# Starting the recurrent heads inside the second half's projections, one step per half tile, matmuls kept in program order

## The chip, the cores and the metric

The kernel runs on one core of one Trainium2 chip. The metric is device time in microseconds (us) of one execution; lower is better. Before the change three runs took 2574.16, 2576.18 and 2580.22 us, median 2576.18.

## The reference, cut to what matters

One inference step of a two-layer hybrid decoder, model width 1024, for 512 prompt rows and 8 sample rows (520 columns in the kernel). A layer is a half-step SwiGLU FFN, a token mixer and another half-step FFN, each followed by a residual layer norm. The mixer projects its input with one wide matrix and splits the columns among sliding-window attention, a Mamba-2 branch and HGRN2, a gated linear recurrence; each branch is projected, gated, summed, and projected once more.

The change is about HGRN2, which has 4 heads of width 128:

```
qh = silu(q);  f = lb + (1 - lb) * sigmoid(f_logit);  kh = (1 - lb) * sigmoid(-f_logit)
o_t = q_t . S_t        with  S_t = diag(f_t) S_(t-1) + k_t i_t^T      (per head, 512 steps)
y = rmsnorm(o) * silu(g)
```

The 512 steps are worked out in blocks instead of one by one: products of f inside blocks of 8, then pair products q k^T in five levels of block sizes 8, 8, 16, 32 and 64 with q and k rescaled between levels, then a state for each 128 steps. The 8 sample rows take one step each from a stored state.

## The kernel before, in words

Activations lie transposed: 8 tiles of 128 features by 520 columns, in two halves of 260 columns. Every large product is done in three matmuls on a high and a low part (`gemm`, L177 to L179), 8 tiles deep, so one unit of output (128 columns of the weight) for one half is 24 matmuls: a "half tile". A weight tile is 512 KB; it is loaded by a DMA on SP's queue (L87), and split into high part by ScalarE (L90) and low part by VectorE (L91).

An instruction's place in its engine's queue is settled at compile time by a scheduler that follows dependencies and priorities; `early(k)` raises the priority of what is traced inside it as if it had been traced some thousand instructions sooner (`EARLY`). At run time each engine works through its queue in order, and an instruction waits on semaphores for its inputs. `keep_in_program_order` adds an order, without a semaphore, between an instruction and the one traced before it on its engine.

In `mixer` (L557) the work around the change is:

- `hgrn_lin` (L601) projects 16 units: 0 to 3 are the four f_logit tiles T (identity evacuation, L517), then for each head q (SiLU, L526 to L528), i (identity) and g (SiLU). The ten units of `MIX_HEAD` (L501) are done for the first half of the columns, and then all ten for the second half, with their weight tiles loaded again; `ln_rest` puts the second half of the layer norm behind the third unit. The other six units, and then six units of `attention_lin` (L1083), have both halves in one go.
- `weave` (L585) takes one full unit of projections per round, and behind it, under `early(3)`, `pace` steps of every live head. A head is a generator (`hgrn_head`, L633), and a step is what lies between two `yield`s. `HG_ROUNDS` and `HG_SAMPLES` say in which round a head, or a sample head (`hgrn_sample`, L760), begins. Before, the rounds begin behind both halves of `MIX_HEAD`: 12 rounds of two steps each.
- A head's steps: **setup** (two sigmoids on ScalarE, L639 and L640, scalings on VectorE, a chain of 6 and one of 5 products on POOL, L652 and L655, and a reciprocal, L653); **scaling** of q and k (L660, L661) into `hep` and `hk`; **levels**, each 8 matmul instructions into a bank of tag "s" (L678), a masked copy (L693, L688 or L683), and a rescaling of both operands for the next level (L697 and L698 behind level 0, L705 and L706 behind the others); **transposes** of i and k (L717, L718); the **state** (L724, L725, L728); the **output** (L735, L738), its norm (L743 to L746); its **transpose** (L754), gating (L756) and split.
- A sample head copies its columns (L765), transposes them (L769), stores them to DRAM (L773, r8d), reads them back spread over the partitions (L779), and updates the state on POOL and VectorE (L780 to L789).
- `merge` (L1273) for branch 0 comes next; its second product needs the split outputs of all four heads.

Tag "s" has 3 PSUM banks, tag "g" of the projections 4, and a head's wide tiles come from 8 slots (`sum_slot`).

Of the kernel before, what the change touches and what calls it, by code (L numbers as in the profile page):

```python
# [15 lines left out]
AF = mybir.ActivationFunctionType  # L16
# [3 lines left out]
P = 128  # L20
# [23 lines left out]
HK = DT // 2  # L44
HG_ROUNDS = (0, 2, 4, 5)
AT_ROUNDS = (0, 0, 3, 3)
HG_SAMPLES = (5, 6, 8, 10)

# [77 lines left out]
class Kernel:  # L126
# [373 lines left out]

    MIX_HEAD = (0, 1, 2, 3, 4, 5, 6, 7, 8, 9)  # L501

# [3 lines left out]

    def lin(self, evac, m=P, halves=(0, 1)):
        wt = self.w.get()
        for half in halves:
            c0, c1 = HALVES[half]  # L510
            p = self.bank()
            self.gemm(p, wt, self.xs, half, m=m)
            with self.early(1):
                evac(p[:m, : c1 - c0], c0, c1)

    def lin_bias(self, out, bias, scale=1.0, halves=(0, 1)):
        self.lin(lambda p, c0, c1: self.nc.scalar.activation(out[:, c0:c1], p, AF.Identity, bias=bias, scale=scale), halves=halves)  # L517

    def lin_silu(self, out, hbias, halves=(0, 1)):

        nc = self.nc

        def evac(p, c0, c1):
            u = self.half_tile()[:, : c1 - c0]
            t = self.half_tile()[:, : c1 - c0]
            nc.scalar.activation(u, p, AF.Identity, bias=hbias, scale=0.5)  # L526
            nc.scalar.activation(t, p, AF.Tanh, bias=hbias, scale=0.5)
            nc.vector.scalar_tensor_tensor(out[:, c0:c1], t, 1.0, u, op0=ALU.add, op1=ALU.mult)  # L528

        self.lin(evac, halves=halves)  # L530

# [25 lines left out]
    def mixer(self, l):  # L557
# [5 lines left out]
        lins = self.hgrn_lin(l)  # L563
# [5 lines left out]
        pair = lambda i: self.attention_pair(l, i, aq)  # L569

        starts = [(r, head(h)) for h, r in enumerate(HG_ROUNDS)] + [(r, smp(h)) for h, r in enumerate(HG_SAMPLES)]
        self.weave(lins, starts, 22 - len(self.MIX_HEAD), 2)
        with self.early(3):
# [25 lines left out]


    def hgrn_lin(self, l):  # L601
        nc = self.nc
        pr, dp, sp = self.par[l], self.dp[l], self.sp
        T = [self.slot(name="hT") for _ in range(HGH)]
        q, it, sg = {}, {}, {}

        def unit(u, halves=(0, 1)):
            hb = dp[:, u : u + 1]
            if u < 4:
                self.lin_bias(T[u], pr[:, 48 + u : 49 + u], halves=halves)  # L610
                return
            h, kind = (u - 4) // 3, (u - 4) % 3
            d, n = ((q, "hq"), (it, "hi"), (sg, "hsg"))[kind]
            if h not in d:
                d[h] = self.slot(name=n)
            if kind == 1:
                self.lin_bias(d[h], pr[:, 48 + u : 49 + u], halves=halves)
            else:
                self.lin_silu(d[h], hb, halves)

        for half in (0, 1):
            for u in self.MIX_HEAD:
                unit(u, (half,))
                if half == 0 and u == 2:
                    self.ln_rest()
        yield T, q, it, sg
        for u in range(16):
            if u in self.MIX_HEAD:
                continue
            unit(u)  # L630
            yield

    def hgrn_head(self, l, h, st):  # L633
# [36 lines left out]
        def level(i):  # L670
# [42 lines left out]
        for src, dst in ((it[h], itok), (ks, ktok)):  # L713
            p = self.bank("s")
            for c in range(4):
                cs = slice(c * P, (c + 1) * P)
                nc.tensor.transpose(p[:, cs], src[:, cs], self.ident)  # L717
            nc.scalar.copy(dst[:, :TP], p)  # L718
# [3 lines left out]
        for c in range(4):  # L722
            cs = slice(c * P, (c + 1) * P)
            nc.tensor.matmul(pst[:, cs], lhsT=ktok[:, cs], rhs=itok[:, cs], start=True, stop=True)  # L724
        nc.vector.tensor_copy(st[:, :P], pst[:, :P])  # L725
# [7 lines left out]
        for c in range(4):  # L733
            cs = slice(c * P, (c + 1) * P)
            nc.tensor.matmul(po[:, cs], lhsT=att[:, c, :], rhs=itok[:, cs], start=c == 0, stop=False)  # L735
        for c in range(1, 4):
            cs, ps = slice(c * P, (c + 1) * P), slice((c - 1) * P, c * P)
            nc.tensor.matmul(po[:, cs], lhsT=qp[:, cs], rhs=st[:, ps], start=False, stop=c == 3)  # L738
        o = self.sum_slot("ho")[:, :TP]
# [9 lines left out]
        )  # L749
        yield  # L750
        pt = self.bank("s")
        for c in range(4):
            cs = slice(c * P, (c + 1) * P)
            nc.tensor.transpose(pt[:, cs], o[:, cs], self.ident)  # L754
        yv = self.sum_slot("hy")[:, :TP]
# [4 lines left out]
    def hgrn_sample(self, l, h, st):  # L760
# [3 lines left out]
        for n, t in zip(("q", "i", "sg"), st[1:]):  # L764
            nc.vector.tensor_copy(sp[n][:, sl], t[h][:, TP:])  # L765

        p = self.bank("x")
        for k, n in enumerate(("f", "k", "q")):
            nc.tensor.transpose(p[:8, k * P : (k + 1) * P], sp[n][:, sl], self.ident)  # L769
        r8 = self.sm(3 * P, "r8", rows=8)  # L770
# [111 lines left out]
    def mamba(self, l):  # L882
# [16 lines left out]
        for j in range(4):  # L899
            self.lin_silu(z[j], dp[:, 28 + j : 29 + j])  # L900
            nc.vector.tensor_copy(self.sp["z"][:, 8 * j : 8 * j + 8], z[j][:, TP:])
# [181 lines left out]
    def attention_lin(self, l, aq):  # L1083
        nc = self.nc
        pr = self.par[l]
        k = self.slot(name="ak")
        self.lin_bias(k, pr[:, 48 + 16 : 48 + 17])
        nc.vector.tensor_copy(self.sp["ak"][:, :8], k[:, TP:])
        nc.sync.dma_start(self.ap["o_pk"][l], k[:, TP - P : TP])
        yield  # L1090
        v = self.slot(name="av")
        self.lin_bias(v, pr[:, 48 + 17 : 48 + 18])
# [3 lines left out]
        yield  # L1096
        for i in range(4):
            q = self.slot(name="aq")
            self.lin_bias(q, self.qb[l][:, i : i + 1], scale=0.125)
            nc.vector.tensor_copy(self.sp["aq"][:, 8 * i : 8 * i + 8], q[:, TP:])  # L1100
            aq[i] = q
            yield

# [456 lines left out]
```

## Time and profile before

| | |
|---|---|
| three runs, median | 2576.18 us (2574.16 to 2580.22) |
| profiled execution | 2577.91 us, of which 2576.1 us are the span from first to last instruction |
| mean granted TensorE clock | 0.993 |
| TensorE matmul, weight load | 98%, 96% of the span |
| VectorE, ScalarE, POOL | 76%, 49%, 27% |
| DMA | 318 MB, mean 124 GB/s |

The two layers run one after the other. In layer 0 the mixer's projections begin near 369 us, their second half near 399, and the first merge near 540; in layer 1 the same work comes 1278 us later. In the profile's names, `g` and `s` are PSUM banks by tag, `hk` a head's scaled key, `hep` its scaled query, `hst` its state, `smp` and `s_q` to `s_sg` tiles of the samples, `wh` and `wl` the weight parts. A wait row says which engine and line waited, on which engine's tile and line, for how long in total, how often, and the longest.

### The profile page before, as it was taken

What the parts mean: (1) busy time and instruction counts of PE and PEld (TensorE: products, weight loads), DVE (VectorE), ACT (ScalarE), POOL (GpSimd) and SP (SyncE); (2) the same over time, 40 slices, a digit from 0 to 9 for tenths busy, and PEclk for the clock granted to TensorE, in tenths of its full rate; (3) what the DMA queues carried; (4) which work ended last, traced back from release to release, by engine and by line L of the source; (5) the groups of instructions that cost most, each with busy time, mean ns of one, the idle gap of its engine ahead of it and who ended that gap; (6) DMA issues with size and microseconds to landing.
All of it is one profiled execution on the core that took longest, in us unless ns stands there. A gap on an engine that the chain in (4) does not pass through costs nothing.

```text
span 2576.1 us, 51903 instructions
## 1 busy us (share of the span) xinstructions
PE 2513.6 (98%) x20784; PEld 2471.3 (96%) x20784; DVE 1948.8 (76%) x3690; ACT 1255.2 (49%) x2366; POOL 694.1 (27%) x645
## 2 busy tenths in 40 slices
PE   8999999999999999999999999999999999999997
PEld 8999999899989999999989999998999899899997
DVE  8795988865594598858897858988646846979596
ACT  6352566444534463435563434764445345635255
POOL 2121243400143432312331212433001434412124
PEclk9999999999999999999999999999999999999999
DMA  6332356522342433232542414564233433433233
GB/s 210 106 127 76 130 180 217 153 67 89 114 133 85 138 129 110 83 115 90 194 126 85 146 57 145 172 222 140 70 104 99 129 99 128 132 101 119 79 120 119
DMA packets 134066, 318.17 MB, mean 124 GB/s; under 512 B 20452, under 2 KB 56516, under 8 KB 133824
## 3 DMA queue, kind: packets, MB, share of 16 engines
q1 hardware_dynamic: 133824, 314.86, 37.6%
q8 instruction: 163, 2.67, 0.4%
q14 instruction: 79, 0.65, 0.1%
HBM read 302.93 MB, written 11.88 MB: 122 GB/s over the span
## 4 chain that ended last, share of the span: by engine, by line
PE 73%; DVE 15%; DMA 4%; issue 3%; POOL 3%; ACT 2%; SPq 0%; POOLq 0%; ACTq 0%; DVEq 0%
PE g L178 15%; PE g L177 15%; PE g L179 15%; PE g L409 6%; PE g L411 5%; PE g L410 5%; DVE wl L91 3%; PE s L409 2%; PE s L411 2%; PE s L410 2%; DMA ws<-in_w_gu 1%; DVE y L249 1%; DMA smp<-r8d 1%; DVE xl L253 1%; DVE wl L74 1%
## 5 line engine op out<-in xcount | busy, mean ns | idle before, releaser
L177 PE MATMUL g<-xh,wh 128*128 128x260 f32 (+1 forms) x2336 | 668.4, 287 | 6.7 <-ACT xh L1423 5.7
L178 PE MATMUL g<-xl,wh 128*128 128x260 f32 (+1 forms) x2336 | 668.3, 286 | 3.6 <-DVE xl L253 2.7
L179 PE MATMUL g<-xh,wl 128*128 128x260 f32 (+1 forms) x2336 | 667.6, 286 | 1.9 <-DVE wl L91 1.9
L90 ACT CAST wh<-ws 128x1024 fp32r<-128x1024 f32 (+1 forms) x382 | 390.0, 1025 | 348.7 <-PE g L178 228.8
L91 DVE TENSOR_TENSOR wl<-ws,wh 128x1024 fp32r<-128x1024 f32 (+1 forms) x382 | 466.2, 1223 | 109.2 <-ACT wh L90 108.2
L177 PEld LDWEIGHTS g<-xh,wh 128*128 128x128 f32 (+1 forms) x2336 | 438.5, 188 | 10.2 <-ACT xh L1423 5.7
L178 PEld LDWEIGHTS g<-xl,wh 128*128 128x128 f32 (+1 forms) x2336 | 438.4, 188 | 9.3 <-DVE xl L253 4.2
L179 PEld LDWEIGHTS g<-xh,wl 128*128 128x128 f32 (+1 forms) x2336 | 438.7, 188 | 6.5 <-DVE wl L91 3.4
L73 ACT CAST wh<-ws 128x1024 fp32r<-128x1024 f32 (+1 forms) x288 | 265.4, 942 | 300.4 <-PE g L178 161.8
L179 PE MATMUL g<-hh,wl 128*128 128x260 f32 x1408 | 395.9, 283 | 0.0
L178 PE MATMUL g<-hl,wh 128*128 128x260 f32 x1408 | 395.7, 283 | 0.0
L177 PE MATMUL g<-hh,wh 128*128 128x260 f32 x1408 | 392.6, 283 | 1.9 <-DVE y L275 1.9
L74 DVE TENSOR_TENSOR wl<-ws,wh 128x1024 fp32r<-128x1024 f32 (+1 forms) x288 | 321.1, 1121 | 86.9 <-ACT wh L73 85.6
L105 POOL TENSOR_TENSOR ws<-ws 128x512 f32<-128x512 f32 x72 | 132.3, 1837 | 635.1 <-DMA ws<-in_w_gu 281.8
L179 PEld LDWEIGHTS g<-hh,wl 128*128 128x128 f32 x1408 | 264.8, 188 | 0.2
L177 PEld LDWEIGHTS g<-hh,wh 128*128 128x128 f32 x1408 | 262.7, 188 | 2.4 <-DVE y L275 2.3
L178 PEld LDWEIGHTS g<-hl,wh 128*128 128x128 f32 x1408 | 264.7, 188 | 0.1
L409 PE MATMUL g<-xh,wh 128*128 128x260 f32 x864 | 245.8, 285 | 2.9 <-ACT wh L73 2.5
L410 PE MATMUL g<-xl,wh 128*128 128x260 f32 x864 | 243.8, 283 | 0.0
L411 PE MATMUL g<-xh,wl 128*128 128x260 f32 x864 | 241.5, 282 | 1.9 <-DVE wl L74 1.9
L409 PEld LDWEIGHTS g<-xh,wh 128*128 128x128 f32 x864 | 163.3, 189 | 5.8 <-ACT wh L73 4.4
L409 PE MATMUL g<-sx,wh 128*128 128x260 f32 x576 | 164.2, 285 | 4.3 <-ACT wh L73 4.3
(411 smaller groups left out, 5727.5 us busy)
## 6 DMA issues: line engine op xcount, KB each, us to landing
ws<-in_w_gu SPq DMA_DIRECT2D x208, 512.0 KB
ws<-in_w_in SPq DMA_DIRECT2D x132, 512.0 KB
ws<-in_w_dn SPq DMA_DIRECT2D x96, 512.0 KB
ws<-in_w_out SPq DMA_DIRECT2D x32, 512.0 KB
ws<-in_w_dn SPq DMA_DIRECT2D x32, 384.0 KB
smp<-r8d SPq DMA_DIRECT2D x48, 256.0 KB
ws<-in_w_br SPq DMA_DIRECT2D x24, 512.0 KB
smp<-in_hgr SPq DMA_DIRECT2D x16, 256.0 KB
```

Source lines behind the costliest of these rows:

```text
L73: nc.scalar.copy(h[:, :n], s[:, :n])
L74: nc.vector.tensor_tensor(lo[:, :n], s[:, :n], h[:, :n].bitcast(F32), op=ALU.subtract)
L90: nc.scalar.copy(h[:, :n], s[:, :n])
L91: nc.vector.tensor_tensor(lo[:, :n], s[:, :n], h[:, :n].bitcast(F32), op=ALU.subtract)
L105: nc.gpsimd.tensor_tensor(pa[:, b], u[:, a], u[:, b], op=ALU.add)
L177: nc.tensor.matmul(out, lhsT=h[:, wc], rhs=xh[:, c0:c1], start=st, stop=False)
L178: nc.tensor.matmul(out, lhsT=h[:, wc], rhs=xl[:, c0:c1], start=False, stop=False)
L179: nc.tensor.matmul(out, lhsT=lo[:, wc], rhs=xh[:, c0:c1], start=False, stop=en)
L249: nc.vector.scalar_tensor_tensor(y, y, gn, rb, op0=ALU.mult, op1=ALU.mult)
L409: nc.tensor.matmul(out, lhsT=h[:, wc], rhs=xh, start=first and k == 0, stop=False, **go)
L410: nc.tensor.matmul(out, lhsT=h[:, wc], rhs=xl, start=False, stop=False, **go)
L411: nc.tensor.matmul(out, lhsT=lo[:, wc], rhs=xh, start=False, stop=k == HK - 1, **go)
```

## The change

The heads and samples are woven in from the second half of `MIX_HEAD` on. A round is now a half tile and takes one step of each live head: 10 + 24 = 34 rounds. The `lin` helpers become generators that yield behind every half tile. Heads begin in rounds 2, 6, 10 and 15, samples in 14, 18, 22 and 27. `MIX_HEAD` is reordered so that head 0's q, i and g come right behind its T, and head 1's behind these. A head has two empty steps between setup and scaling, a new step border between level 0 with its rescaling and level 1, and two empty steps ahead of the last transpose; a sample has a new border between copies and transposes. All matmuls and transposes of heads and samples go through `keep_in_program_order`. No instruction is added or removed.

```diff
-HG_ROUNDS = (0, 2, 4, 5)
+HG_ROUNDS = (2, 6, 10, 15)
-HG_SAMPLES = (5, 6, 8, 10)
+HG_SAMPLES = (14, 18, 22, 27)
...
-    MIX_HEAD = (0, 1, 2, 3, 4, 5, 6, 7, 8, 9)
+    MIX_HEAD = (0, 4, 5, 6, 1, 7, 8, 9, 2, 3)
...
-    def lin(self, evac, m=P, halves=(0, 1)):
+    def lin(self, *args, **kw):
+        for _ in self.lin_steps(*args, **kw):
+            pass
+
+    def lin_steps(self, evac, m=P, halves=(0, 1)):
...
                 evac(p[:m, : c1 - c0], c0, c1)
+            yield
...
-        self.weave(lins, starts, 22 - len(self.MIX_HEAD), 2)
+        self.weave(lins, starts, len(self.MIX_HEAD) + 2 * (22 - len(self.MIX_HEAD)), 1)
+        for _ in lins:
+            pass
...
+    def mm(self, *args, **kw):
+        self.tc.keep_in_program_order(self.nc.tensor.matmul(*args, **kw))
+
+    def tr(self, *args):
+        self.tc.keep_in_program_order(self.nc.tensor.transpose(*args))
...
-        for half in (0, 1):
-            for u in self.MIX_HEAD:
-                unit(u, (half,))
-                if half == 0 and u == 2:
-                    self.ln_rest()
+        for u in self.MIX_HEAD:
+            for _ in unit(u, (0,)):
+                pass
+            if u == self.MIX_HEAD[2]:
+                self.ln_rest()
         yield T, q, it, sg
+        for u in self.MIX_HEAD:
+            yield from unit(u, (1,))
         for u in range(16):
-            if u in self.MIX_HEAD:
-                continue
-            unit(u)
-            yield
+            if u not in self.MIX_HEAD:
+                yield from unit(u)
...
             nc.gpsimd.tensor_tensor(rv[:, :, a], f[:, :, b], rv[:, :, b], op=ALU.mult)
+
+        yield
+        yield
         yield
         qp, ks = self.sum_slot("hep")[:, :TP], ks[:, :TP]
...
-                nc.tensor.matmul(
+                self.mm(
                     out.rearrange("p (b w) -> p b w", w=w) if i else out,
...
         nc.vector.tensor_tensor(em3, em3, ts.unsqueeze(2).to_broadcast([P, 64, 8]), op=ALU.mult)
         w = 8
+        yield
         for i in range(1, 5):
...
             op=ALU.mult,
         )
         yield
+        yield
+        yield
         pt = self.bank("s")
...
             nc.vector.tensor_copy(sp[n][:, sl], t[h][:, TP:])
+        yield
 
         p = self.bank("x")
```

The other matmuls and transposes of `hgrn_head` and `hgrn_sample` change to `self.mm` and `self.tr` in the same way, and `attention_lin` and the z projections of `mamba` call the generators.

## Rows read from the trace of the kernel before

**Rows 1.** The page, part 1: busy time, share of the span and instructions of each engine.
```profile
PE 2513.6 (98%) x20784; PEld 2471.3 (96%) x20784; DVE 1948.8 (76%) x3690; ACT 1255.2 (49%) x2366; POOL 694.1 (27%) x645
```

**Rows 2.** TensorE's waits, whole kernel: us in total, times, longest us.
```profile
PE s L678 <- DVE hk L698: 7.2, 5, 2.5
...
PE s L678 <- DVE hk L706: 4.0, 6, 1.2
...
PE x L769 <- DVE s_q L765: 2.3, 2, 1.2
...
PE s L738 <- DVE hst L725: 1.5, 2, 1.0
...
PE s L678 <- DVE s_sg L765: 0.8, 1, 0.8
...
PE s L724 <- ACT hkt L718: 0.5, 1, 0.5
PE s L754 <- DVE ho L746: 0.4, 1, 0.4
```

**Rows 3.** Stretches of both layers: us, busy us (instructions) by engine, granted clock, DMA share, GB/s.
```profile
400.00:560.00 160.00, 152.12 (x1262) 148.64 (x1262) 124.20 (x315) 81.71 (x225) 49.92 (x62) 0.99 0.51 157
500.00:530.00 30.00, 27.54 (x224) 26.55 (x223) 26.13 (x78) 12.18 (x42) 5.77 (x5) 0.94 0.44 135
530.00:560.00 30.00, 30.00 (x254) 29.92 (x253) 15.45 (x54) 13.39 (x35) 1.04 (x2) 1.00 0.23 73
514.00:517.40 3.40, 3.40 (x20) 2.82 (x19) 3.32 (x10) 1.48 (x10) 0.00 (x0) 0.51 0.15 30
...
1678.00:1838.00 160.00, 151.20 (x1268) 148.01 (x1268) 124.92 (x315) 82.69 (x226) 50.00 (x62) 1.00 0.50 158
```

**Rows 4.** TensorE's timeline, 511 to 515.5: start, us, line, tiles, count [idle before <- releaser].
```profile
512.38 1.08 PE L678 MATMUL s<-hep,hk 128*128 128x64 f32 x8 [2.46 <-DVE hk L698]
...
513.47 0.28 PE L177 MATMUL g<-xh,wh 128*128 128x260 f32 x1
513.59 0.28 PE L178 MATMUL g<-xl,wh 128*128 128x260 f32 x1
...
514.49 0.42 PE L178 MATMUL g<-xl,wh 128*128 128x260 f32 x1
514.70 0.42 PE L179 MATMUL g<-xh,wl 128*128 128x260 f32 x1
```

**Rows 5.** The same table for instructions of L177 alone (8 in each half tile).
```profile
398.60:450.80 52.20, 34.01 (x120) 22.40 (x119) 1.00 0.74 235
...
398.60:553.90 155.30, 87.33 (x306) 57.74 (x305) 0.99 0.52 161
```

**Rows 6.** VectorE's timeline, 393 to 397: end of the layer norm.
```profile
395.08 0.88 DVE L253 SCALAR_TENSOR_TENSOR xl<-y,par,xh 128x260 fp32r<-128x260 f32 x2
```

**Rows 7.** Timelines of ACT and VectorE, 402 to 416: head 0's setup.
```profile
402.65 0.47 ACT L517 ACTIVATE hT<-g,par 128x260 f32<-128x260 f32 x1
...
415.45 0.43 DVE L661 TENSOR_TENSOR hk<-hk,hrv 128x256 f32<-128x256 f32 x1 [0.52 <-POOL hrv L655]
```

**Rows 8.** VectorE's and POOL's timelines, 428 to 431, and L705's instructions of the whole kernel.
```profile
428.70 1.20 DVE L705 TENSOR_TENSOR hep<-hep,tw 128x256 f32<-128x256 f32 x1
...
428.32 1.30 POOL L780 TENSOR_TENSOR smp<-smp 128x512 f32<-128x512 f32 x1
...
L705 DVE TENSOR_TENSOR hep<-hep,tw x32: 410/418/1495, 428.7 to 1807.4; 128x256 f32<-128x256 f32 x32
```

**Rows 9.** VectorE's groups, 400 to 560: line, tiles, count, busy us, mean ns, idle before.
```profile
L91 DVE TENSOR_TENSOR wl<-ws,wh 128x1024 fp32r<-128x1024 f32 x25 | 31.0, 1244 | 4.2 <-ACT wh L90 4.2
L783 DVE SCALAR_TENSOR_TENSOR smp<-smp,s_i 128x128 f32<-128x128 f32 x32 | 9.5, 352 | 5.5 <-POOL smp L780 2.9 <-DMA smp<-r8d 2.6
...
L528 DVE SCALAR_TENSOR_TENSOR hsg<-ht 128x260 f32<-128x260 f32 x7 | 3.2, 457 | 3.7 <-ACT ht L527 3.7
```

**Rows 10.** SP's timeline, 421 to 422: DMA issues.
```profile
421.34 0.35 SPq L773 DMA_DIRECT2D r8d<-r  x1
```

More of the change, by code (lines that the diff above doesn't have):

```diff
@@ L514, in lin @@
                 evac(p[:m, : c1 - c0], c0, c1)
+            yield
     def lin_bias(self, out, bias, scale=1.0, halves=(0, 1)):
-        self.lin(lambda p, c0, c1: self.nc.scalar.activation(out[:, c0:c1], p, AF.Identity, bias=bias, scale=scale), halves=halves)
+        return self.lin_steps(
+            lambda p, c0, c1: self.nc.scalar.activation(out[:, c0:c1], p, AF.Identity, bias=bias, scale=scale), halves=halves
+        )
     def lin_silu(self, out, hbias, halves=(0, 1)):
@@ L528, in evac @@
             nc.vector.scalar_tensor_tensor(out[:, c0:c1], t, 1.0, u, op0=ALU.add, op1=ALU.mult)
-        self.lin(evac, halves=halves)
+        return self.lin_steps(evac, halves=halves)
     def split(self, y, name, slot=None):
@@ L609, in unit @@
             if u < 4:
-                self.lin_bias(T[u], pr[:, 48 + u : 49 + u], halves=halves)
-                return
+                return self.lin_bias(T[u], pr[:, 48 + u : 49 + u], halves=halves)
             h, kind = (u - 4) // 3, (u - 4) % 3
@@ L616, in unit @@
             if kind == 1:
-                self.lin_bias(d[h], pr[:, 48 + u : 49 + u], halves=halves)
-            else:
-                self.lin_silu(d[h], hb, halves)
-        for half in (0, 1):
-            for u in self.MIX_HEAD:
-                unit(u, (half,))
-                if half == 0 and u == 2:
-                    self.ln_rest()
+                return self.lin_bias(d[h], pr[:, 48 + u : 49 + u], halves=halves)
+            return self.lin_silu(d[h], hb, halves)
+        for u in self.MIX_HEAD:
[3 more added lines that the diff above has]
+                self.ln_rest()
         yield T, q, it, sg
+        for u in self.MIX_HEAD:
+            yield from unit(u, (1,))
         for u in range(16):
-            if u in self.MIX_HEAD:
-                continue
-            unit(u)
-            yield
+            if u not in self.MIX_HEAD:
+                yield from unit(u)
     def hgrn_head(self, l, h, st):
@@ L716, in hgrn_head @@
                 cs = slice(c * P, (c + 1) * P)
-                nc.tensor.transpose(p[:, cs], src[:, cs], self.ident)
+                self.tr(p[:, cs], src[:, cs], self.ident)
             nc.scalar.copy(dst[:, :TP], p)
@@ L723, in hgrn_head @@
             cs = slice(c * P, (c + 1) * P)
-            nc.tensor.matmul(pst[:, cs], lhsT=ktok[:, cs], rhs=itok[:, cs], start=True, stop=True)
+            self.mm(pst[:, cs], lhsT=ktok[:, cs], rhs=itok[:, cs], start=True, stop=True)
         nc.vector.tensor_copy(st[:, :P], pst[:, :P])
@@ L734, in hgrn_head @@
             cs = slice(c * P, (c + 1) * P)
-            nc.tensor.matmul(po[:, cs], lhsT=att[:, c, :], rhs=itok[:, cs], start=c == 0, stop=False)
+            self.mm(po[:, cs], lhsT=att[:, c, :], rhs=itok[:, cs], start=c == 0, stop=False)
         for c in range(1, 4):
             cs, ps = slice(c * P, (c + 1) * P), slice((c - 1) * P, c * P)
-            nc.tensor.matmul(po[:, cs], lhsT=qp[:, cs], rhs=st[:, ps], start=False, stop=c == 3)
+            self.mm(po[:, cs], lhsT=qp[:, cs], rhs=st[:, ps], start=False, stop=c == 3)
         o = self.sum_slot("ho")[:, :TP]
@@ L753, in hgrn_head @@
             cs = slice(c * P, (c + 1) * P)
-            nc.tensor.transpose(pt[:, cs], o[:, cs], self.ident)
+            self.tr(pt[:, cs], o[:, cs], self.ident)
         yv = self.sum_slot("hy")[:, :TP]
@@ L765, in hgrn_sample @@
             nc.vector.tensor_copy(sp[n][:, sl], t[h][:, TP:])
+        yield
         p = self.bank("x")
         for k, n in enumerate(("f", "k", "q")):
-            nc.tensor.transpose(p[:8, k * P : (k + 1) * P], sp[n][:, sl], self.ident)
+            self.tr(p[:8, k * P : (k + 1) * P], sp[n][:, sl], self.ident)
         r8 = self.sm(3 * P, "r8", rows=8)
@@ L899, in mamba @@
         for j in range(4):
-            self.lin_silu(z[j], dp[:, 28 + j : 29 + j])
+            for _ in self.lin_silu(z[j], dp[:, 28 + j : 29 + j]):
+                pass
             nc.vector.tensor_copy(self.sp["z"][:, 8 * j : 8 * j + 8], z[j][:, TP:])
@@ L1086, in attention_lin @@
         k = self.slot(name="ak")
-        self.lin_bias(k, pr[:, 48 + 16 : 48 + 17])
+        yield from self.lin_bias(k, pr[:, 48 + 16 : 48 + 17])
         nc.vector.tensor_copy(self.sp["ak"][:, :8], k[:, TP:])
         nc.sync.dma_start(self.ap["o_pk"][l], k[:, TP - P : TP])
-        yield
         v = self.slot(name="av")
-        self.lin_bias(v, pr[:, 48 + 17 : 48 + 18])
+        yield from self.lin_bias(v, pr[:, 48 + 17 : 48 + 18])
         nc.vector.tensor_copy(self.sp["av"][:, :8], v[:, TP:])
@@ L1095, in attention_lin @@
         aq["k"], aq["v"] = k, v
-        yield
         for i in range(4):
             q = self.slot(name="aq")
-            self.lin_bias(q, self.qb[l][:, i : i + 1], scale=0.125)
+            yield from self.lin_bias(q, self.qb[l][:, i : i + 1], scale=0.125)
             nc.vector.tensor_copy(self.sp["aq"][:, 8 * i : 8 * i + 8], q[:, TP:])
             aq[i] = q
-            yield
     def by_group(self, t):
```

## The prediction

> **What bounds the kernel now.** The page's engine line comes first [rows 1]: TensorE is busy 2513.6 of 2576.1 us, so only its idle time, some 62 us, and any time at a low clock can be won; the change removes no matmul. The waits of TensorE over the whole kernel come next [rows 2]. Seven of the entries belong to the recurrent heads (L678, L724, L738, L754) and their samples (L769): 7.2 + 4.0 + 2.3 + 1.5 + 0.8 + 0.5 + 0.4 = 16.7 us. The table of stretches puts them [rows 3]: between the mixer's second-half projections and the first merge TensorE is busy 152.12 of 160 us in layer 0 and 151.20 of 160 in layer 1, so 7.88 + 8.80 = 16.7 us are idle there, the same sum. VectorE is busy 124.20 of 160 in that stretch, but 26.13 of 30 where the heads are densest and 15.45 of 30 behind that. So the stage is TensorE's, held up in places where a head's matmul stands in its queue before VectorE has finished the input.
>
> TensorE's timeline shows such a place [rows 4]: the second level of a head waits 2.46 us for L698, and behind it the spacing of the projections' matmuls goes from 0.12 to 0.21-0.22 us. The stretch from 514.0 to 517.4 has a granted clock of 0.51, the 1.2 GHz level [rows 3]: at half speed its 3.4 us held 1.7 us of work, so 1.7 us were lost.
>
> **The change, part by part.** A half tile is 24 matmuls at 0.12 us [rows 4], 2.9 us. The projections' second half begins near 398.7 us, and L177 (8 in a half tile) counts the half tiles since then [rows 5]: head 1's first level stands at 120 / 8 = 15, head 3's last transpose (553.9) at 306 / 8 = 38. The stretch of 155 us holds 918 of these matmuls and about 36 of the merge, 114 us; less 7.9 us idle and 1.7 us of low clock, the heads' own matmuls take some 31 us, 7.8 a head. The change keeps them all; only their places and the waits in front of them count.
>
> *Order of the projections.* Units 4, 5, 6 now follow unit 0. In the first half this brings one or two SiLU evacuations (two ACTIVATE of 0.47 us, one VectorE operation of 0.42) ahead of the rest of LN's second half. The last xl of LN ends at 395.96 [rows 6], 2.7 us before TensorE needs the second half. I cost it at nothing; if that margin is gone, at most 1.4 us a layer. The weights are listed in the same order, with the same number of loads.
>
> *Heads' setup.* Head 0's chain from its T (evacuated at 402.65) through ACT's table load, the six and five POOL products, to its scaled key ends at 415.88 [rows 7], 17.2 us after the second half begins. Under the new plan level 0 of head 0 comes behind seven half tiles, 20.2 us. The two empty steps cover it, at cost 0; without them level 0 would stand behind five half tiles, 14.4 us, and wait some 3 us.
>
> *The levels.* Every head now has a half tile between level 0 with its two scalings (L697, L698) and level 1. The five waits for L698 make 7.2 us and the longest is 2.5 [rows 2], shorter than a half tile: I take all 7.2 off. Between later levels VectorE has a masked copy, L705 and L706, three operations like L705's median of 0.42 us [rows 8], 1.3 us together, and often a weight split of 1.24 [rows 9]; 2.5 us just fit into 2.9. Of the 4.0 us for L706 I take half off, 2.0. The waits for hst, hkt and ho (1.5 + 0.5 + 0.4) lie behind longer chains; half off, 1.2.
>
> *Samples.* The new step between their copies and their transposes takes off the two waits for s_q, 2.3, and the one for s_sg, 0.8. Their DMAs move past weight loads on SP's in-order queue: layer 0's first r8d store was issued at 421.34 [rows 10] and can now come only behind half tile 16, some 453 us. That is eleven DMAs a head, moved out of the part in which each half tile loads its own weight tile. The seven entries already make the stage's whole idle time [rows 2, 3], so none of it is a wait for weights and the loads have slack; cost 0. Were that cover gone, a weight load held behind a sample's read would cost a few us once a layer. POOL's two products per half sample (one took 1.3 us [rows 8]) move likewise; only the sample waits for them.
>
> *Pins.* They are an order and no semaphore: a head's matmul may not stand ahead of the projections traced before it, but may stand behind later ones. Each adds nothing of its own. What stands behind a late one is the whole of TensorE's queue, as before.
>
> *Low clock.* It followed the 2.46 us wait; with that gone, 1.7 us come back.
>
> *What is late next.* The plan wants the heads earlier: head 1's level 0 behind 11 half tiles instead of 15, head 3's end behind 30 instead of 38. VectorE's load per head is at most (124.2 - 31.0 - 9.5 - 5.9) / 4 = 19.5 us, the stage less weight splits, sample products and 13 SiLU operations at 0.457 us, 7 of which the row shows [rows 3, 9], or 1.3 us for each of 15 rounds. In rounds 15 to 20 three heads are live: 3.9 us, half a split (0.6), SiLU and samples (0.5), 5.0 us of VectorE against 2.9 + 3 x 7.8 / 15 = 4.4 us of TensorE. That is 0.6 us short in each of six rounds, 3.6 us a layer if nothing slips and 0 if the plan's matmuls slip behind later projections; I take 3 a layer, nearer the first because the matmuls already stood ahead of their inputs before. Sum: -7.2 - 2.0 - 1.2 - 2.3 - 0.8 - 1.7 + 6 = **-9.2 us**. Bounds of the whole: all waits and the low clock gone, -18.4; from above, the second rival.
>
> The profiled execution took 2577.9 us, 1.8 beyond its span and 1.7 above the median of 2576.2. I set the difference against the median: 2567.
>
> **The rivals.** *No binding pin, no change.* All bounds but head 0's first lie earlier than where the matmuls stood, so a pin that only forbids moving ahead may bind nothing: the queue's order is again what the scheduler thinks ready, and VectorE is again late by the same 5%. For it: head 1's level 0 stood four half tiles behind its new bound without any pin [rows 5]. Against: the steps that waited longest get a half tile each. The samples' 3.1 us go, new waits give about as much back: 2574 to 2578, near 2576.
>
> *VectorE takes over (slower).* The place is rounds 15 to 20, where the heads' scalings, the weight splits and POOL's products of the next head meet. For it: VectorE was busy 87% in the densest stretch [rows 3], and L705 took 1.20 us at 428.70, while POOL worked from 428.32 on, instead of its usual 0.42 [rows 8]. If the named waits only change their names, the 16.7 us stay and 3.6 us a layer are added: 2576 + 7 = 2583, and up to 3 us more if each layer gets a low-clock stretch of its own. It decides once VectorE is busy over some 97% of those six rounds. Against: a third of VectorE's time was free in the 30 us behind the dense part.
> The Trainium skill, page "SBUF — State Buffer", section "Who interferes with whom", says that a VectorE instruction with two SBUF inputs contends with a GpSimd instruction that reads SBUF, and its section "SBUF: two separate sides" calls the shared port pair a lock held for the whole instruction. L705 has two such inputs, and its 1.20 us beside POOL's product agree; by that rule alone, packing one head's POOL setup beside two others' levels speaks against the change, towards this rival's time.
>
> **How the numbers follow.** Two runs of this kernel can be told apart at about 0.2%, 5.2 us. The forecast, 2559 to 2571, gets 0.53; no change 0.25; VectorE's rival 0.22. The forecast lies on the side of faster; a weak form of the second and third falls within 0.2%. So faster 0.53, same 0.26, slower 0.21. The range takes the forecast's best side to 2559 and goes up into the third case, to 2584, leaving some 2 in 10 out.
>
> **What would show it.** Right: no wait of L678 for L698 left above 0.5 us, none of L769 for s_q; TensorE idle in the two stages 8 us or less instead of 16.7; no low clock there; the last head transpose near half tile 30 to 34. Wrong: waits of L678 for L706 or L697 of several us between half tiles 15 and 25 with VectorE at 97% or more (the third case), or the levels at the same half tiles as before with the same waits (the second). A new wait of a projection on xl at the start of the second half would show the cost of the new unit order; one on wl, a weight load held on SP's queue.

## The result and the profile after

The kernel after took 2599.72 us (2595.84 to 2604.40, four runs) and the kernel before 2577.73 on the same chip: a ratio of 1.0081, 95% interval 1.0067 to 1.0095. It is slower by some 21 us, above the range and on the other side of the forecast. The profiled execution took 2596.74 us, with a span of 2595.0 against 2576.1, 18.9 us more.

First the table of stretches in layer 0 (us, busy us and instructions of PE, PEld, DVE, ACT, POOL, then granted clock, DMA share, GB/s), of the kernel before and then of the one after:
```profile
400.00:520.00 120.00, 112.12 (x923) 108.94 (x923) 100.92 (x233) 64.59 (x181) 48.89 (x60) 0.99 0.60 185
520.00:580.00 60.00, 60.00 (x493) 59.13 (x492) 37.50 (x132) 27.29 (x75) 1.04 (x2) 1.00 0.20 65
```
```profile
400.00:520.00 120.00, 118.24 (x1007) 116.56 (x1006) 97.94 (x242) 65.00 (x162) 35.30 (x53) 1.00 0.45 146
520.00:580.00 60.00, 49.94 (x363) 45.28 (x363) 36.16 (x131) 27.68 (x102) 12.79 (x9) 0.86 0.44 136
...
532.40:535.80 3.40, 3.40 (x18) 3.40 (x17) 2.00 (x11) 1.14 (x8) 0.61 (x1) 0.50 0.70 156
546.10:556.30 10.20, 5.91 (x16) 4.70 (x17) 6.07 (x20) 3.41 (x11) 2.71 (x2) 0.50 0.49 159
563.10:566.50 3.40, 3.29 (x14) 2.79 (x15) 2.87 (x11) 3.40 (x19) 0.00 (x0) 0.50 0.00 0
```
Where the heads are dense the change did what it was meant to do: TensorE's idle time fell from 7.88 to 1.76 us. Behind that, where there was none, 10.06 us appeared, and the granted clock fell to 0.86. Its three low stretches are 17.0 us long, and TensorE was busy in 12.6 of them: at half speed 6.3 us were lost, against 1.7 before. (An idle microsecond at a low clock counts once, as idle.) That is +3.9 idle and +4.6 of clock, 8.5 us in layer 0. The same count in layer 1 gives +4.6 and +4.8, so 17.9 of the 18.9 us stand here. Counted from the last product of the first FFN to the last product of the first merge, the mixer grew from 271.4 to 283.4 us in layer 0 and from 270.2 to 283.1 in layer 1, and what follows it shrank by 3.4 and 2.5: 8.6 and 10.4 us net, 19.0 in all.

TensorE's waits over the whole kernel of after answer to [rows 2] (all matmuls of heads and samples now have L612, their transposes L615; L1166 and L1201 are the attention's scores and transposes, which weren't in that list):
```profile
PE s L1166 <- DVE hy L777: 6.4, 2, 3.7
PE s L1201 <- DVE asc L1191: 4.6, 2, 2.4
PE s L612 <- DVE hk L725: 3.7, 8, 0.7
PE s L612 <- DVE hst L747: 3.7, 4, 1.3
PE s L1166 <- DVE am L1172: 3.6, 2, 2.1
PE s L615 <- DVE ho L765: 2.1, 2, 1.3
```
The wait behind level 0 and those of the samples are gone. New ones, of the attention, make 14.6 us, all behind 520 in layer 0 and behind the like place in layer 1.

TensorE's timeline there (start, us, line, tiles, count [idle before <- releaser]):
```profile
542.70 0.28 PE L181 MATMUL g<-xh,wl 128*128 128x260 f32 x1
544.24 0.63 PE L615 MATMUL s<-ident,ho 128*128 128x128 f32 x4 [1.26 <-DVE ho L765]
...
548.26 1.62 PE L1166 MATMUL s<-att,aq 128*128 128x128 f32 x4 [2.73 <-DVE hy L777]
...
552.83 2.08 PE L1166 MATMUL s<-att,aq 128*128 128x256 f32 x4 [2.12 <-DVE am L1172]
...
563.21 2.64 PE L1201 MATMUL s<-ident,asc 128*128 128x128 f32 x11 [2.20 <-DVE asc L1191]
565.83 0.58 PE L179 MATMUL g<-yhh,wh 128*128 128x260 f32 x1
566.21 0.42 PE L179 MATMUL g<-xh,wh 128*128 128x260 f32 x1
```
From 542.7 to 565.8 the projections and the merge stand still but for three matmuls, and TensorE has little but the attention's, whose groups wait for VectorE. From 546.1 on, inside the second of these gaps, the granted clock is at the 1.2 GHz level for 10.2 us. What they waited for shows on VectorE, in its waits from 520 to 566:
```profile
DVE smp L805 <- POOL smp L802: 11.1, 3, 5.0
DVE asc L1172 <- DMA abias<-in_c_abias: 2.6, 1, 2.6
```
VectorE's own queue is held by the samples' accumulations, which wait for POOL, with `hy` and the attention behind them. The second row is the load of the attention's bias, and it leads to the samples too. On SP's timeline it was issued right behind the store of a sample's state:
```profile
547.52 0.34 SPq L806 DMA_DIRECT2D out_o_shg<-smp  x1
547.96 0.87 SPq L1152 DMA_DIRECT2D abias<-in_c_abias  x2
```
That store had itself waited 2.8 us for the accumulations on VectorE. And the samples are late: before, the first one's transposes stood at 407.96, now at 469.24, near half tile 20, on TensorE's timelines of before and after:
```profile
407.96 0.27 PE L769 MATMUL x<-ident,s_f 128*8 128x128 f32 x1
```
```profile
469.24 0.27 PE L615 MATMUL x<-ident,s_f 128*8 128x128 f32 x1
469.35 0.27 PE L615 MATMUL x<-ident,s_k 128*8 128x128 f32 x1
469.46 0.27 PE L615 MATMUL x<-ident,s_q 128*8 128x128 f32 x1
```
ACT's last sample work (L789 before, L811 after) ends at 515.2 before and 552.3 after, and VectorE writes the last sample columns of the heads' outputs (L553) only by 566.9:
```profile
562.48 0.25 DVE L823 SCALAR_TENSOR_TENSOR s_o<-s_o,par,s_sg 128x32 f32<-128x32 f32 x1
...
566.62 0.31 DVE L553 TENSOR_TENSOR yhl<-s_o,yhh 128x8 fp32r<-128x8 f32 x3
```
The second-half products of the first merge read columns 260 to 520, the 8 sample columns among them, and TensorE's queue is in order. So a merge product that can't begin holds back what stands behind it.

### The profile page after: what moved, and what is told of

Same layout as the page of the kernel before. It is cut to its first block, busy times and chain, and to the rows that moved or that the text cites. A ratio compares the mean times of both kernels' runs of the same rounds, so it can differ in the third digit from the quotient of the medians.

```text
span 2595.0 us, 51912 instructions
## 1 busy us (share of the span) xinstructions
PE 2526.4 (97%) x20784; PEld 2478.0 (95%) x20784; DVE 1941.0 (75%) x3690; ACT 1256.4 (48%) x2366; POOL 692.9 (27%) x645
## 5 line engine op out<-in xcount | busy, mean ns | idle before, releaser
L179 PEld LDWEIGHTS g<-xh,wh 128*128 128x128 f32 (+1 forms) x2336 | 439.4, 188 | 10.2 <-ACT xh L1443 5.6
```

Of the source, the lines that this page charges most:

```text
L179: nc.tensor.matmul(out, lhsT=h[:, wc], rhs=xh[:, c0:c1], start=st, stop=False)
```

## The experiments

Each result below is a median, then the ratio to the kernel before, taken on the same chip, with its 95% interval.

### Which part makes the bunch

The bunch is the stretch from 542.7 to 565.8. Theory S: the pinned samples come late and block the first merge. P: the pins on the heads make the bunch. W: the samples' DMAs on SP hold up the merge's weights.

**Sample transposes unpinned** in the kernel after:
```diff
-            self.tr(p[:8, k * P : (k + 1) * P], sp[n][:, sl], self.ident)
+            nc.tensor.transpose(p[:8, k * P : (k + 1) * P], sp[n][:, sl], self.ident)
```


> The changed kernel, but the samples' transposes are no longer kept in program order; heads stay as changed. Theory S (the pinned samples finish late, the first merge's second-half product needs their columns, PSUM banks of tag g are given out in order, so the merge's matmuls stop and TensorE has only attention matmuls that wait on VectorE, at 1.2 GHz): the samples go back to half tiles 3 to 20, the bunched attention block near 543 to 566 us goes, and what the heads' new plan saved is left: 2563 to 2574 us. Rival P (the pins on the heads' own matmuls and the earlier heads make the bunch; samples are incidental): 2592 to 2603 us. Rival W (the samples' DMAs on SP's queue hold back the merge's weights): as theory S.

Measured: 2592.65 us, 1.0049 (1.0032 to 1.0067). The bunch went, but only 8 of the 21 us; by its time the run lies in P's range, not in S's. The stretches say why:
```profile
400.00:520.00 120.00, 110.67 (x921) 108.49 (x920) 102.11 (x244) 65.34 (x186) 50.05 (x61) 0.99 0.58 184
520.00:580.00 60.00, 60.00 (x491) 59.16 (x490) 36.03 (x125) 28.27 (x80) 0.76 (x2) 1.00 0.23 74
430.00:460.00 30.00, 27.12 (x229) 26.44 (x229) 28.46 (x60) 16.26 (x50) 18.02 (x22) 1.00 0.65 206
```
With the samples early again POOL does 50 us instead of 35 ahead of 520, and TensorE idles 9.33 us there, more than before the change. Over the whole kernel three of its waits tell what became of the levels:
```profile
PE s L612 <- DVE hk L725: 10.2, 9, 2.9
PE x L791 <- DVE s_f L657: 8.1, 4, 2.3
...
PE s L612 <- DVE hk L716: 0.2, 1, 0.2
```
The wait behind level 0 (L716, L698 before) stays away. But the wait for the later rescalings (L725, L706 before) grew from 4.0 to 10.2, and one for a copy of the samples, s_f, is new: in the two stages (some 220 us of each layer) TensorE idles 23.0 us instead of 16.7.

**No pins at all** (`mm` and `tr` call the plain instructions):


> The changed kernel with no matmul or transpose kept in program order; the start rounds, empty steps and unit order stay. Theory S: the samples are early again, so no bunch: 2565 to 2580 us, with waits of the levels back in the stage 400 to 530. Rival P: 2570 to 2580 us. This run tells what the pins on the heads are worth by the difference to the kernel with unpinned samples: 3 to 8 us by theory S.

Measured: 2595.35 us, 1.0056 (1.0039 to 1.0073), not to be told from the run above, and above both ranges. In this plan the pins on the heads neither make nor cure the loss: P falls for the kernel after.

**Sample columns kept out of the merge's way**, in the kernel after; this leaves the sample rows' HGRN2 output out and puts gate columns in its place:
```diff
-        self.hg_out.append(self.split(yv, "yh"))
+        yh, yl = self.split(yv, "yh")
+        nc.scalar.copy(yh[:, TP:], sg[h][:, TP:])
+        nc.vector.tensor_tensor(yl[:, TP:], sg[h][:, TP:], yh[:, TP:].bitcast(F32), op=ALU.subtract)
+        self.hg_out.append((yh, yl))
...
-        self.split_samples(o, self.hg_out)
```


> The changed kernel, pins and all, but the sample columns of the heads' split outputs are copied from the gate tile at the end of each head instead of coming from the samples' output step; the sample rows' HGRN2 result is left out of the merge. The samples' work and their DMAs stay as late as in the changed kernel. Theory S: the merge no longer waits for the samples, attention is interleaved with projections again: 2565 to 2578 us. Rival W (weights held on SP's queue) and rival P (pins on heads): still 2592 to 2603 us.

Measured: 2587.26 us, 1.0027 (1.0018 to 1.0036). The samples are as late as in after and have the same DMAs, but nothing of the merge waits for them: 0.54%, 14 us, come back. That is two thirds of the loss, less than S expected; the run stops between the two ranges. W falls for the merge's weights. SP's queue still shows on the attention's bias: VectorE waits 3.0 us for that load in this run too.

**Only the samples' transposes pinned, in the kernel before:**
```diff
-            nc.tensor.transpose(p[:8, k * P : (k + 1) * P], sp[n][:, sl], self.ident)
+            self.tc.keep_in_program_order(nc.tensor.transpose(p[:8, k * P : (k + 1) * P], sp[n][:, sl], self.ident))
```


> The kernel before, with one thing changed: the samples' transposes are kept in program order, with the start rounds of before. Theory S: the samples' transposes slip from half tiles 3 to 24 to 21 and later, the merge stops for them, 1.2 GHz stretches near 545 and 563 us: 2590 to 2606 us. Rival P: nothing of note, 2573 to 2581 us. Rival W: as theory S.

Measured: 2620.46 us, 1.0153 (1.0137 to 1.0168): twelve transposes a layer pinned where the plan of before has them cost 40 us. TensorE's longest wait and a stretch of the same run:
```profile
PE s L754 <- DVE ho L746: 28.6, 2, 14.9
```
```profile
549.60:570.10 20.50, 6.59 (x23) 5.68 (x24) 11.25 (x37) 6.72 (x35) 5.06 (x4) 0.50 0.56 175
```
The last head's norm waited 5.7 us for ACT, which itself stood 6.2 us at a sample's product on POOL, and then stood in VectorE's queue among the samples' accumulations, one of which waited 2.48 us for POOL; the whole stretch had the 1.2 GHz level. That is above S's range. That late samples cost this much is shown, though here by the queues of ACT and VectorE more than by the merge.

### Other places for the samples and the heads

**Samples pinned earlier**, in the kernel after: `HG_SAMPLES = (6, 10, 16, 22)`.


> HG_SAMPLES goes from (14, 18, 22, 27) to (6, 10, 16, 22); everything else is the kernel after, pins included. Theory S (late samples hold up the first merge, 12 to 13 us by the runs without sample columns) expects part of that back: the samples' last transposes stand some 5 half tiles earlier, the merge's second half is blocked for less time: 2584 to 2592, with less than 5 us of low clock between 520 and 610. Theory V (a second cause: the heads begun 4 to 8 half tiles earlier pack VectorE between 400 and 470) expects the waits for hk to come back there as the samples' VectorE and POOL work moves in: TensorE under 28 of 30 us in 430:460 or 460:490, so not below 2584. If V is wrong and the samples are the whole cause, 2575 to 2582.

Measured: 2599.22 us, 1.0083 (1.0068 to 1.0098): nothing gained. Idle time moved from behind 520 (10.06 us in after, 3.50 here from 520 to 580) to 430:490, where TensorE was busy 26.06 and 26.67 of 30. S alone had expected less; what the samples don't cost late they cost early.

**The same, with the first merge in pairs of units,** the first-half products of two units ahead of their second-half products:
```diff
+                for half in (0, 1):
+                    c0, c1 = HALVES[half]
+                    w = c1 - c0
+                    for n in (n0, n0 + 1):
```


> As the run with samples pinned early, and the first merge takes its units in pairs, with the first-half products of both units ahead of the second-half products, so that gemms that don't need the sample columns lie between the attention's matmuls for longer. Same arithmetic and the same loads in another order. Theory S (the second half of the merge is what the sample columns block) expects 3 to 8 us less than the run with samples pinned early, 2576 to 2588, and no stretch of 3 us at 1.2 GHz between 520 and 610. If the block is not the merge's order, the two are equal within 3 us.

Measured: 2600.59 us, 1.0082 (1.0066 to 1.0099), no change: with the samples here the order of the merge is not the limit.

**Only the heads pinned, in the kernel before** (their matmuls and transposes as `self.mm` and `self.tr`).


> The kernel before, with the heads' matmuls and transposes pinned in TensorE's queue and the samples left free. Theory V with S: pins on the heads alone do no harm (with the plan of after, taking them away cost 2 to 3 us), the samples stay early, the heads start where they did: 2571 to 2580. Theory P (a pinned head's matmul makes a bunch behind it) expects waits behind late heads' matmuls and low clock: 2585 to 2600.

Measured: 2598.67 us, 1.0077 (1.0060 to 1.0094): a miss for V with S, inside P's range. Without pins the scheduler had put head 0's first level at 419.8, ahead of its traced place; pinned, it came at 440.3, and everything behind it later.

**Heads begun later**, in the kernel after with samples free: `HG_ROUNDS = (8, 12, 16, 20)`.


> The kernel after with the samples' transposes free (as in the run that took their pins away, 2592.65 us) and HG_ROUNDS at (8, 12, 16, 20) instead of (2, 6, 10, 15): new unit order, half-tile steps, empty steps and the heads' pins stay, and the heads begin about where they did before. Theory V (the earlier heads pack VectorE) expects most of the 14 us that this kernel stands above the one before back: 2574 to 2584, TensorE at 28.5 or more of 30 us in 430:460 and 460:490. Rival U (the unit order, the half-tile steps or the split of the levels' first step cost it, wherever the heads begin) expects 2588 to 2595.

Measured: 2594.75 us, 1.0063 (1.0048 to 1.0078). Level 0 of head 0 came at 444.0, not at the 419.8 of before, so this run is no return to the old places; it shows only that heads some 25 us later than in the kernel after (level 0 at 418.7) don't help either.

### One part of the change at a time

**The unit order alone**, in the kernel before: `MIX_HEAD = (0, 4, 5, 6, 1, 7, 8, 9, 2, 3)`.


> The kernel before with the unit order of after alone: the first ten units as 0, 4, 5, 6, 1, 7, 8, 9, 2, 3, and LN's second half after the third of them. Plan, steps, samples as before, no pin. The prediction costed this part at nothing, at most 1.4 us a layer: 2576 to 2582. Theory U (the new order brings head 0's and head 1's inputs sooner and so sends the samples' copies, POOL's products and the heads' setup into the same stretch of VectorE, 400 to 470): 2586 to 2595, with waits for s_f or newton between 400 and 470 and VectorE over 27 of 30 us in 430:460.

Measured: 2584.52 us, 1.0022 (1.0013 to 1.0032): 5.7 us, some 3 a layer, more than "nothing" and less than theory U expected. U's place doesn't show: VectorE was busy 20.81 of 30 us in 430:460. What its trace has more of in the stage is low clock (a granted 0.90 in 430:460, where before had 1.00); why is open.

**The level's step border alone**, in the kernel before with head 3 begun in round 6:
```diff
         nc.vector.tensor_tensor(em3, em3, ts.unsqueeze(2).to_broadcast([P, 64, 8]), op=ALU.mult)
         w = 8
+        yield
```


> As the level step alone, with head 3 begun one round later (HG_ROUNDS (0, 2, 4, 6)), so that no head overwrites an attention tile that another has still to read, and the result is that of the kernel before. If the step's split saves what the prediction took off: 2568 to 2574. If nothing binds: 2576 to 2582. If splitting the step costs by itself, as the first run of it seems to say: 2586 to 2594.

Measured: 2587.96 us, 1.0035 (1.0019 to 1.0050): slower, and the wait for L698 stays (3.0 us from 395 to 585, longest 2.7). A border in an unpinned plan changes priorities and forbids nothing, which would fit; that is argued, not tested, and head 3's round moved as well. With head 3 in its old round (the first run of it, where head 3's attention tile was written ahead of head 1's last read) it took 2592.63.

**The plan of before, no pins,** in the kernel after, without the empty steps: `HG_ROUNDS = (10, 14, 18, 22)`, `HG_SAMPLES = (20, 22, 26, 30)`.


> As the plan of before without pins, with head 3 begun two rounds later (HG_ROUNDS (10, 14, 18, 22)), so that no attention tile is overwritten early. Theory V2 (the earlier plan costs most of the 16 us of the run without pins; the unit order, 5 us, stays): 2580 to 2586. If the half-tile steps or the split first step cost it: 2588 to 2597.

Measured: 2589.80 us, 1.0040 (1.0028 to 1.0052), against 1.0056 with the new plan, so the earlier plan isn't the main cost. What is left, 0.40%, is no more than the unit order (0.22%) and the split step (0.35%) cost alone; they weren't taken out together, so its cause stays open. The first run of it, with head 3 in round 20 and the same overwriting, took 2589.55.

### The two kernels without their samples

```diff
         p = self.bank("x")
-        for k, n in enumerate(("f", "k", "q")):
...
+        nc.vector.tensor_copy(sp["o"][:, sl], st[1][h][:, TP:])
+        yield
```


> The kernel before without the samples' recurrent step: no transposes, no DMAs, no products on POOL and VectorE for them; a copy of the gate columns stands in for their output, and the sample states aren't written. A control for the next run. Theory V (the samples' VectorE and POOL work is what makes heads wait): the stage's 16.7 us of idle over two layers falls by half or more, 2562 to 2572. If the samples are hidden: 2572 to 2578.

> The kernel after with the same left out. Against the control it shows the heads' part of the change, with unit order, half-tile steps, plan and pins, alone. Theory S with V (the heads' part is good by itself and only the samples, late and blocking or early and crowding VectorE, make it lose): at or below the control by up to 10 us, 2555 to 2568, with no low clock between 520 and 610. Rival H (the heads' part itself loses, by earlier starts or by the pins): 5 to 15 us above the control.

Measured: 2556.37 us for the kernel before, 0.9908 (0.9892 to 0.9924), and 2560.17 for the one after, 0.9925 (0.9908 to 0.9942). The first 120 us of the stage, before and then after:
```profile
400.00:520.00 120.00, 120.00 (x1024) 118.86 (x1023) 90.22 (x235) 60.36 (x133) 26.90 (x45) 1.00 0.32 105
```
```profile
400.00:520.00 120.00, 119.09 (x1017) 118.02 (x1016) 96.48 (x249) 61.05 (x135) 26.05 (x45) 1.00 0.32 104
```
This is the run that the others led to. With its old plan and no pin, the kernel before never waits for a head: TensorE is busy 120.00 of 120 us, and its idle time in the two stages is 0.1 us instead of 16.7. The change of the heads has nothing to win there; it is 3.8 us behind, between the two ranges, which the intervals don't quite tell apart. The samples cost 23.8 us before (2580.2 - 2556.4) and some 40 after (1.0081 - 0.9925 = 1.56% of 2580).

### Why the samples cost so much

The runs without samples take away their work on every engine and their DMAs at once. Theory Q: their instructions in VectorE's queue wait for POOL and for reads, with the heads' behind them. C: POOL's products slow VectorE's instructions beside them.

**Accumulation off VectorE,** first in the kernel before, then in the kernel after with samples free:
```diff
-                nc.vector.scalar_tensor_tensor(s3[:, b], kb[:, b], sp["i"][:, c : c + 1], s3[:, b], op0=ALU.mult, op1=ALU.add)
+                nc.scalar.activation(kb[:, b], kb[:, b], AF.Copy, scale=sp["i"][:, c : c + 1])
+            nc.gpsimd.tensor_tensor(s3, s3, kb, op=ALU.add)
```


> The kernel before with the samples' accumulation moved from VectorE (32 instructions a layer, 0.34 to 0.6 us each, some of them waiting for POOL's product or for a read of r8d) to ACT (a scaled copy for each) and one POOL addition of 1.3 us for each half sample. Same result. Theory Q (the samples' instructions in VectorE's queue hold up the heads' scalings): half or more of the 24 us that the samples cost come back, 2560 to 2570, TensorE at 29 or more of 30 us in 430:460 and 490:520. Theory C (POOL's products slow VectorE's instructions beside them): POOL has eight products more a layer, so no gain or a loss, 2576 to 2590.

> The kernel after with its samples' transposes free (2592.65 us as it was) and the same move of the samples' accumulation off VectorE. Theory Q: 2560 to 2574, within 6 us of the same move made in the kernel before, since the heads' part of the change was worth +4 us without samples. Theory C: 2590 or more.

Measured: 2595.94 us, 1.0064 (1.0049 to 1.0079), and 2596.72, 1.0069 (1.0052 to 1.0086). VectorE has 32 instructions a layer fewer, and the first kernel gets slower (16 us, above C's range), while the second is not to be told from its like with samples free. In the first, POOL is busy 59.1 us from 400 to 520 (48.9 before) and VectorE 99.4 (100.9 before): what was taken off it went into slower instructions, as C says. ACT has more to do as well, 73.6 us against 64.6, so this run alone doesn't decide.

**POOL's products on VectorE,** in the kernel before:
```diff
-            nc.gpsimd.tensor_tensor(s3, s3, fb, op=ALU.mult)
+            nc.vector.tensor_tensor(s3, s3, fb, op=ALU.mult)
...
-            nc.gpsimd.tensor_tensor(qb, qb, s3, op=ALU.mult)
+            nc.vector.tensor_tensor(qb, qb, s3, op=ALU.mult)
```


> The kernel before with the samples' two products of each half sample on VectorE instead of POOL: 16 instructions of 128x512 a layer, an estimated 0.6 us each from VectorE's 1.22 us for 128x1024, 10 us of VectorE a layer more, 24 us of POOL a layer less. Theory C (POOL beside VectorE is what the samples cost most by): 2562 to 2576, VectorE's masked copies near 0.42 us, fewer waits for hk. Theory Q (VectorE's in-order queue, held by samples that wait for their DMA): VectorE waits for the reads itself now, 2580 to 2600.

Measured: 2572.68 us (2568.04 to 2577.44, ten runs), 0.9971 (0.9958 to 0.9985): **faster than both kernels**, with 11 us more of work on VectorE a layer (16 instructions of 0.69). VectorE's groups from 400 to 520 (line, tiles, count, busy us, mean ns, idle before) show it on the levels' rescalings; the kernel before, before without samples, with POOL's extra additions, with the products on VectorE:
```profile
L705 DVE TENSOR_TENSOR hep<-hep,tw 128x256 f32<-128x256 f32 x13 | 8.3, 635 | 0.0
L706 DVE TENSOR_TENSOR hk<-hk,tw 128x256 f32<-128x256 f32 x13 | 6.1, 468 | 0.0
```
```profile
L705 DVE TENSOR_TENSOR hep<-hep,tw 128x256 f32<-128x256 f32 x16 | 6.8, 427 | 3.0 <-PE s L678 3.0
```
```profile
L705 DVE TENSOR_TENSOR hep<-hep,tw 128x256 f32<-128x256 f32 x12 | 7.4, 619 | 0.6 <-PE s L678 0.6
L706 DVE TENSOR_TENSOR hk<-hk,tw 128x256 f32<-128x256 f32 x12 | 7.7, 638 | 0.0
```
```profile
L705 DVE TENSOR_TENSOR hep<-hep,tw 128x256 f32<-128x256 f32 x12 | 5.0, 415 | 0.0
L706 DVE TENSOR_TENSOR hk<-hk,tw 128x256 f32<-128x256 f32 x12 | 5.4, 454 | 0.0
```
The means mix two kinds. Of the 13 L705 of the kernel before ten took 0.41 to 0.42 us and three 1.20, 1.50 and 1.41, each beside a product of the samples on POOL, as this one, on VectorE's and POOL's timelines:
```profile
444.64 1.50 DVE L705 TENSOR_TENSOR hep<-hep,tw 128x256 f32<-128x256 f32 x1
```
```profile
444.57 1.28 POOL L780 TENSOR_TENSOR smp<-smp 128x512 f32<-128x512 f32 x1 [3.70 <-DMA smp<-r8d]
```
With the products on VectorE none of its 32 L705 takes more than 0.42. And VectorE's busy time does not grow by the products' 11 us, it stays where it was (100.92 before):
```profile
400.00:520.00 120.00, 118.18 (x1001) 116.49 (x999) 101.26 (x255) 68.83 (x186) 25.08 (x44) 1.00 0.61 192
```
So C's mechanism is shown: the products on POOL had cost VectorE about as much time as doing them itself does. How much of the gain it makes isn't separated from the waits of VectorE for POOL's products, 2.9 us from 400 to 520, which go as well. That the heads' setup waited behind them in POOL's own queue is not it, since VectorE's waits for the setup's products are 3.0 us before and 2.6 here. Q isn't refuted by this: the samples' instructions now wait 5.6 and 2.6 us on VectorE for reads of r8d, and 16 of the samples' 24 us are still there. How much of those is queueing and how much the work itself was not tried.

## Why the prediction was wrong

The step that failed is the samples' move, which the sum put at 0 (the second point). The others say what became of the rest of the sum.

- **"What bounds the kernel now"** read the waits rightly and their cause wrongly. The 16.7 us of idle time stood at heads' matmuls, so the text took them for a matter of the heads' order alone. Without samples the same heads in the same plan wait for nothing. A wait row names the late producer, not what made it late.
- **The samples' move, costed at 0**, is the step that failed: "only the sample waits for them" overlooks three followers. The merge's second-half products read the sample columns (14 us by the run that keeps them out; the first transposes came at 469.24, where the text had the store behind them at some 453), and VectorE's queue takes the samples' accumulations in line (11.1 us of waits for POOL between 520 and 566). The third is SP's queue, which the text did name as a risk, but for weights. The waits for weight parts stayed as they were (for `wl` 1.9 us before, 1.8 after); the attention's bias is what came late there, 2.6 us of VectorE's time.
- **The levels, -7.2 - 2.0 - 1.2.** The wait behind level 0 did go, with the samples free too (0.2 us), but that for the later rescalings went only from 4.0 to 3.7, and hst and ho grew from 1.9 to 5.8 with L747 and L765. The total did not fall by the step: with the samples early TensorE's idle time from 400 to 520 is 9.33, the waits having moved to the later rescalings and the samples' copies, and on its own, with head 3 a round later, the border cost 8 to 9 us. After has 1.76 there because the samples' work was pushed behind 520.
- **Low clock, -1.7,** had the wrong sign: it moved from one stretch of 3.4 us to three of 17 us in all in layer 0, and 6.3 us were lost there instead of 1.7.
- **Unit order, 0** (or at most 1.4 a layer): 5.7 us alone, 3 a layer, above the bound; the margin of 2.7 us that the text looked at was not shown to be the reason.
- **Pins, "each adds nothing of its own"**: they bind where the scheduler had moved an instruction ahead of its traced place. Pinning twelve sample transposes a layer cost 40 us, the heads 20, in the plan of before; in that of after, with the samples free, the pins on the heads made no difference that can be told.
- **The rivals.** "No binding pin" falls. "VectorE takes over" has the sign but neither place nor mechanism: VectorE was busy 97.94 us of 120, 82%, where the rival asked for 97%, and the +6 that the sum itself took for a VectorE that is late hardly showed ahead of 520 (1.76 us idle). With the samples free the rival comes close: 23.0 us of idle time instead of 16.7, and VectorE busy 28.46 of 30 us, 95%, in 430:460. Against the rival the text said that a third of VectorE's time was free behind the dense part; by its own row, 15.45 busy of 30, it was half. By the heads' part alone, without samples, the change comes to some +4 us, not -9.2.
- **The signs.** No wait on L698 or for s_q: right. Idle time of 8 us or less and no low clock in the stages: wrong, idle time grew to 25.2 us. The last head transpose stands at 544.2, near half tile 37 and not 30 to 34; before it stood at 554.0, and at 566 with the heads pinned, so it had been ahead of its traced place already.

The Trainium skill, "SBUF — State Buffer", section "Who interferes with whom", has VectorE and GpSimd contend for one port pair. The prediction gave that rule to the slower rival for the heads' setup; the rows agree with it (0.42 us alone against 1.20 to 1.50 beside a product), but for the samples' products, and in the kernel before already.

## What to carry to other kernels

Ahead of moving an instruction, follow its output to the end: the latest consumer here was a merge three generators further on, and the engines on the way (VectorE in line, POOL beside it) had other customers. A pin turns a scheduler's freedom into the traced order, so compare it with where the instruction stood in the trace, not with where the plan puts it. Before a stage's order is tuned, leave out one of its two interleaved kinds of work: that run would have shown at once that the heads wait only beside the samples.

## What the runs showed of the hardware

Beside a product of 128x512 on POOL, which takes 1.3 us, an instruction of VectorE could take about as long as the product: even a copy of 128x8, 0.16 us otherwise, took 1.22. From VectorE's and POOL's timelines of the kernel before:
```profile
432.40 1.22 DVE L765 COPY s_q<-hq 128x8 f32<-128x8 f32 x1
```
```profile
432.21 1.39 POOL L780 TENSOR_TENSOR smp<-smp 128x512 f32<-128x512 f32 x1 [0.91 <-DMA smp<-r8d]
```
It doesn't happen each time: an L705 that began at 438.98 took 0.41 us, 0.02 us behind a product that then took 1.91 instead of 1.3. And the masked copies out of PSUM (L688) took 0.43 us beside a product or not. On VectorE the same product takes 0.69 us, about half. Last, the stretch in which TensorE had only short groups that waited for another engine was paid twice: 4.3 us of its 10.2 were idle in 546.1:556.3, and the rest ran at half speed.
